# A hybrid attention/SSM layer: up projection of two blocks at a time by one level of Strassen's scheme, down summed in PSUM beside late attention

## The chip, the cores and the metric

The kernel runs on one core of one Trainium2 chip. The metric is the device time of one execution in microseconds. The engines are named as in the profile: PE (TensorE), PEld (its weight loads), DVE (VectorE), ACT (ScalarE), POOL (GpSimd) and SP (SyncE, which issues most DMAs).

## The reference, cut to what matters

One layer on 2048 tokens of 1024 channels, all in float32. Attention has 8 heads of 64, the state space model 32 groups of 16 channels, and the FFN 2816 channels.

```python
h = rmsnorm(x, g_mix) * (1.0 + sc_m) + sh_m
q, k, v, f_logit, u = split(h @ w_in)
attn = rmsnorm(forgetting_attention(q, k, v, log_sigmoid(f_logit + b_fgate)), g_attn_out)
ssm = rmsnorm(s5_ssm(u, ...), g_ssm_out)
x = x + gt_m * (concatenate([attn, ssm]) @ w_out)
h = rmsnorm(x, g_ffn) * (1.0 + sc_f) + sh_f
gate_pre, val = split(h @ w_up)                     # w_up: 1024 x (2 * 2816)
gate_pre = causal_dwconv(gate_pre, conv_w, conv_b)  # width 3, over tokens
x = x + gt_f * ((silu(gate_pre) * val) @ w_down)    # w_down: 2816 x 1024
return rmsnorm(x, g_final)
```

## The kernel before

Channels lie on partitions and tokens along the free axis. The 2048 tokens are four blocks of 512 (TB). A float32 product is made from two float32r parts of each factor: `hi` is a rounded copy (ACT, L65 for weights) and `lo` the rest (DVE subtraction, L66), and three matmuls (hi*hi, hi*lo, lo*hi) stand for one. One unit of work for TensorE is therefore three matmuls of 128 x 128 weights against 512 columns.

The program runs in stages. First come the input projections and the conditioning vector (to about 344 us), then the SSM with attention of block 0 and the late query/key/value projections (to about 657 us). From there on it goes block by block: the mixer's rows and the output projection (`mix_t`, `out_proj`), the norm (`h2_of`), then the FFN. The FFN takes 22 column tiles i in four groups of 6, 6, 5 and 5 (FFG): `up(h2, i)` makes gate and value of tile i with 24 matmuls each (L1154) from 1024-wide weight slots, applies the convolution and silu on DVE and ACT (L1158 to L1168), and splits the result into `act_hi` and `act_lo` (L1170, L1171); after each group `down` multiplies the group's tiles for each of eight output tiles d (L1186 to L1188) and adds them to `yt[d]` in SBUF (L1190). The output projection of block b+1 stands inside the last group of block b. Attention of blocks 1 to 3 runs beside the FFNs: per head, `att_max` finds row maxima (L875, L880), `att_main` makes the scores (L918, L919), the exponentials (L928) with their two parts (`ph` L929, `pl` L930), and the products with the values (L939, L943), and adds up the row sums (`acc`, L938, on POOL and in part on DVE).

The order on each engine is set by a list scheduler when the kernel is built, which follows the program's order and the priorities given in it. Weights come by SP's queue into two raw buffers, and each split has three `w_hi` and three `w_lo` buffers.

## Time and profile before

| what | value |
|---|---|
| time, median of 3 runs | 2708.53 us (2705.61 to 2710.71) |
| span of the profiled execution | 2704.6 us (its own time apart from the span is not listed) |
| granted TensorE clock, mean | 0.983 |
| PE busy | 2614.1 us, 97% |
| DVE busy | 2045.6 us, 76% |
| ACT busy | 1165.7 us, 43% |
| POOL busy | 682.6 us, 25% |
| DMA | 378.99 MB, mean 140 GB/s |

Matmuls overlap in the pipe, so a listed duration of 0.40 us is not what one costs; the distance between two starts is. A group's row gives count, busy time, mean duration in ns, then the idle time of that engine just before the group's instructions and what ended it.

### The profile page before, as it was taken

How to read it: one execution, taken by the hardware profiler on the slowest of the kernel's cores; microseconds unless marked ns; L12 is line 12 of the kernel's file. 1: busy time of each engine (PE TensorE's matmuls, PEld its weight loads, DVE VectorE, ACT ScalarE, POOL GpSimd, SP SyncE). 2: the span in 40 equal slices, each digit the busy share in tenths (PEclk: the TensorE clock that was granted, in tenths of full speed). 3: DMA queues.
4: the chain of work that ended last, by engine and by line, in shares of the span. 5: the costliest groups of instructions: out<-in, count | busy, mean ns of one | idle time of the engine just before them, and what ended most of it. 6: DMA issues, size and time to landing. Idle time of an engine off the chain costs nothing.

```text
span 2704.6 us, 35904 instructions
## 1 busy us (share of the span) xinstructions
PE 2614.1 (97%) x12600; PEld 2121.8 (78%) x12600; DVE 2045.6 (76%) x3366; ACT 1165.7 (43%) x1929; POOL 682.6 (25%) x602
## 2 busy tenths in 40 slices
PE   6889999989999999999999999999999999999998
PEld 3778887868788888888888888787888887888886
DVE  7997789875787877888978688879787655855555
ACT  3322245564454443455545344554454333423223
POOL 3675132130322221234323022343222101100001
PEclk8889999999999999999999999999999999999999
DMA  7367877566344442343443233434433233322222
GB/s 270 118 210 226 290 248 223 172 193 213 94 123 133 129 132 85 126 147 103 145 140 127 100 99 128 137 106 141 134 121 106 83 102 114 134 94 88 98 99 75
DMA packets 217668, 378.99 MB, mean 140 GB/s; under 512 B 22384, under 2 KB 107248, under 8 KB 217488
## 3 DMA queue, kind: packets, MB, share of 16 engines
q1 hardware_dynamic: 216208, 372.50, 42.6%
q0 software_dynamic: 1280, 4.20, 0.4%
q8 instruction: 100, 1.64, 0.2%
q14 instruction: 80, 0.66, 0.1%
HBM read 319.79 MB, written 56.75 MB: 139 GB/s over the span
## 4 chain that ended last, share of the span: by engine, by line
PE 81%; DVE 11%; DMA 4%; issue 2%; SPq 1%; ACT 1%; POOL 0%; POOLq 0%; DVEq 0%; ACTq 0%
PE ff_ps L1154 35%; PE ff_ps L1133 6%; PE ff_ps L1186 6%; PE ff_ps L1187 6%; PE ff_ps L1188 6%; PE sc_ps L919 2%; PE sc_ps L875 2%; PE o_ps L939 2%; PE sc_ps L918 2%; PE o_ps L943 2%; PE vq_ps L399 2%; PE qs_ps L399 2%; PE qs_ps L366 1%; PE vq_ps L366 1%; DVE w_lo L66 1%
## 5 line engine op out<-in xcount | busy, mean ns | idle before, releaser
L65 ACT CAST w_hi<-w_raw 128x1024 fp32r<-128x1024 f32 (+2 forms) x384 | 367.5, 959 | 526.4 <-PE ff_ps L1154 201.8
L66 DVE TENSOR_TENSOR w_lo<-w_raw,w_hi 128x1024 fp32r<-128x1024 f32 (+2 forms) x384 | 443.4, 1156 | 188.7 <-ACT w_hi L65 184.9
L1154 PE MATMUL ff_ps<-h_lo,w_hi 128*128 128x512 f32 x1408 | 558.9, 397 | 0.7 <-DVE h_lo L320 0.7
L1154 PE MATMUL ff_ps<-h_hi,w_lo 128*128 128x512 f32 x1408 | 558.8, 397 | 0.7 <-DVE w_lo L66 0.7
L1154 PE MATMUL ff_ps<-h_hi,w_hi 128*128 128x512 f32 x1408 | 553.2, 395 | 0.0
L938 POOL TENSOR_TENSOR acc<-acc,pf 128x512 f32<-128x512 f32 (+2 forms) x240 | 308.7, 1286 | 565.2 <-ACT pf L928 556.8
L1154 PEld LDWEIGHTS ff_ps<-h_lo,w_hi 128*128 128x128 f32 x1408 | 265.4, 189 | 62.0 <-DVE h_lo L320 1.8
L1154 PEld LDWEIGHTS ff_ps<-h_hi,w_hi 128*128 128x128 f32 x1408 | 265.9, 189 | 59.6 <-issue 0.3
L1154 PEld LDWEIGHTS ff_ps<-h_hi,w_lo 128*128 128x128 f32 x1408 | 265.0, 188 | 59.1 <-DVE w_lo L66 1.2
L930 DVE TENSOR_TENSOR pl<-pf,ph 128x512 fp32r<-128x512 f32 (+1 forms) x320 | 268.5, 848 | 54.2 <-ACT ph L929 53.4
L276 POOL TENSOR_TENSOR sq_acc<-sq_acc,sq 128x512 f32<-128x512 f32 x77 | 124.2, 1614 | 691.1 <-ACT sq L275 688.0
L1187 PE MATMUL ff_ps<-act_lo,w_hi 128*128 128x512 f32 (+1 forms) x719 | 281.2, 391 | 0.0
L1188 PE MATMUL ff_ps<-act_hi,w_lo 128*128 128x512 f32 (+1 forms) x719 | 280.0, 391 | 0.0
L1186 PE MATMUL ff_ps<-act_hi,w_hi 128*128 128x512 f32 (+1 forms) x719 | 280.0, 393 | 0.0
L928 ACT ACTIVATE pf<-sc_ps 128x512 f32<-128x512 f32 (+1 forms) x320 | 170.8, 543 | 229.3 <-PE sc_ps L919 79.7
L880 DVE TENSOR_REDUCE mx<-sc_ps 128x1 f32<-128x512 f32 (+2 forms) x320 | 193.8, 616 | 44.5 <-PE sc_ps L875 27.1
L929 ACT CAST ph<-pf 128x512 fp32r<-128x512 f32 (+1 forms) x320 | 178.1, 567 | 44.5 <-PE o_ps L939 40.3
L1188 PEld LDWEIGHTS ff_ps<-act_hi,w_lo 128*128 128x128 f32 x719 | 135.4, 188 | 29.9 <-issue 0.3
L1187 PEld LDWEIGHTS ff_ps<-act_lo,w_hi 128*128 128x128 f32 x719 | 135.4, 188 | 29.2
L1186 PEld LDWEIGHTS ff_ps<-act_hi,w_hi 128*128 128x128 f32 x719 | 135.1, 188 | 29.4
L1190 DVE SCALAR_TENSOR_TENSOR yt<-ff_ps,mod_tf,yt 128x512 f32<-128x512 f32 (+1 forms) x99 | 71.9, 731 | 93.2 <-PE ff_ps L1188 93.1
L1166 ACT ACTIVATE gs<-cvt 128x512 f32<-128x512 f32 x88 | 55.6, 632 | 186.7 <-DVE cvt L1164 186.4
(455 smaller groups left out, 5032.7 us busy)
## 6 DMA issues: line engine op xcount, KB each, us to landing
w_raw<-in_w_flat SPq DMA_DIRECT2D x258, 512.0 KB
w_raw<-in_w_flat SPq DMA_DIRECT2D x64, 384.0 KB
kb<-kb SPq DMA_DIRECT2D x80, 256.0 KB
vv<-v SPq DMA_DIRECT2D x80, 256.0 KB
w_raw<-in_w_flat SPq DMA_DIRECT2D x64, 320.0 KB
wada<-in_w_ada SPq DMA_DIRECT2D x32, 512.0 KB
ka<-kb SPq DMA_DIRECT2D x80, 128.0 KB
xt<-in_x SPq DMA_DIRECT2D x16, 512.0 KB
```

Source lines behind the costliest of these rows:

```text
L65: nc.scalar.copy(hi[:, :n], raw[:, :n])
L66: nc.vector.tensor_tensor(out=lo[:, :n], in0=raw[:, :n], in1=hi[:, :n].bitcast(F32), op=ALU.subtract)
L880: V.reduce_max(out=mx[:, s, ch : ch + 1], in_=ps[:, 0:n], axis=AX.X)
L928: A.activation(pf[:, cs], ps[:, cs], AF.Exp)
L929: A.copy(ph[:, cs], pf[:, cs])
L930: V.tensor_tensor(out=pl[:, cs], in0=pf[:, cs], in1=ph[:, cs].bitcast(F32), op=ALU.subtract)
L938: eng.tensor_tensor(out=acc[j][:, cs], in0=acc[j][:, cs], in1=pf[:, cs], op=ALU.add)
L1133: T.matmul(ps, lhsT=lt, rhs=rt, start=(i == 0), stop=(i == 23))
L1154: T.matmul(ps, lhsT=lt, rhs=rt, start=(n == 0), stop=(n == 23))
L1186: T.matmul(ps, lhsT=a, rhs=ah[:, ts], start=(c == 0), stop=False)
L1187: T.matmul(ps, lhsT=a, rhs=al[:, ts], start=False, stop=False)
L1188: T.matmul(ps, lhsT=bb, rhs=ah[:, ts], start=False, stop=(c == n - 1))
```

## The change

The FFN is taken for two blocks at a time. For tile i the up weights are a 2 x 2 block matrix (gate or value, first or second half of the 1024 input channels: a11, a12, a21, a22), and the two blocks' activations are the other factor. In place of eight block products, seven are made (`product`, 12 matmuls each, L1365): of a11, a12, s1, s2, s4, s3 and a22 with the operands b11, b21, t1, t2, b22, t3 and t4. The operands are built once per pair of blocks (`up_operands`, on DVE and POOL, split on ACT and DVE); the weight combinations s1 to s4 once per tile (`up_pair`, four additions on POOL, L1347 to L1352). Sums of products are formed partly in PSUM (banks X and Z, L1365 with `first=False`), partly by copies on ACT (L1374, L1379, L1381, L1387) and additions on DVE (L1377, L1383, L1388, L1391). Convolution and silu then work on 1024 tokens at once (L1395 to L1401), the first tap now on ACT, and both parts of the result go to DRAM (L1407).

The program's stages are now: the input stage as before; the SSM with attention of blocks 0 and 1 and the late projections, merged by a written order of TensorE; `up_stage(0)`: `mix_t` and `out_proj` of blocks 0 and 1, the operands, 22 `up_pair`; `down_stage(0)`: down of blocks 0 and 1, each output tile summed over all 22 tiles in one PSUM bank and evicted once (L1416), with the activations reloaded from DRAM, while attention of blocks 2 and 3 stands between its steps in a written order of TensorE; `up_stage(1)`; `down_stage(1)`, down of blocks 2 and 3. In the last group of block 3 four output tiles are cut in token halves, where three were.

DVE, in the FFN, before: one column tile of one block (`cvt` and `gs` are the convolution's tiles, 512 tokens; `rs_v` and `rs_i` belong to a norm).

```order
L66 TENSOR_TENSOR w_lo<-w_raw,w_hi 128x1024
L1160 COPY carry<-gs 128x2
L1162 TENSOR_SCALAR cvt<-gs,cv 128x512
L1163 SCALAR_TENSOR_TENSOR cvt<-gs,cv,cvt 128x512
L1164 SCALAR_TENSOR_TENSOR cvt<-gs,cv,cvt 128x512
L1167 SCALAR_TENSOR_TENSOR cvt<-gs,cvt 128x512
L984 COPY ss_att<-sc_ps 128x4
L1158 COPY gs<-carry 128x2
L122 TENSOR_SCALAR rs_v<-ss_att 128x4
L1168 SCALAR_TENSOR_TENSOR cvt<-cvt,ff_ps 128x512
```

DVE in the changed kernel, a column tile of two blocks in the first up stage (`s_11880` and `s_11881` are the tiles s1|s2 and s4|s3 of the next column tile, `v_raw` its second weight slot, `vz` the value branch).

```order
L73 TENSOR_TENSOR w_lo<-s_11880,w_hi 128x1024
L1396 SCALAR_TENSOR_TENSOR cvt<-gs,cv,cvt 128x1024
L1397 SCALAR_TENSOR_TENSOR cvt<-gs,cv,cvt 128x1024
L73 TENSOR_TENSOR w_lo<-s_11881,w_hi 128x1024
L1388 TENSOR_TENSOR vz<-up_x,vz 128x512
L1391 TENSOR_TENSOR vz<-up_y,vz 128x512
L1400 SCALAR_TENSOR_TENSOR cvt<-gs,cvt 128x1024
L1377 TENSOR_TENSOR gs<-up_y,gs 128x512
L1401 SCALAR_TENSOR_TENSOR vz<-cvt,vz 128x1024
L73 TENSOR_TENSOR w_lo<-v_raw,w_hi 128x512
L1384 COPY gs<-bcol 128x2
L1405 TENSOR_TENSOR al<-vz,ah 128x1024
```

The weight splits of the next tile now stand between the steps of this tile's convolution, and the split of a22 (`v_raw`) stands behind all of them; in the tile before and after it, it stands ahead of L1401.

TensorE in the changed kernel, the seam between two column tiles in the first up stage (`up_x_11344` is bank X of the tile that ends, `up_x_11483` of the next; `w_hi_11334` is a part of s4|s3, `w_hi_11457` of a11|a12).

```order
L1365 MATMUL up_z_11345<-hh_hi_9589,w_lo_11335 128x512
L1365 MATMUL up_x_11483<-hh_hi_9163,w_hi_11457 128x512
L1365 MATMUL up_x_11483<-hh_lo_9164,w_hi_11457 128x512
L1365 MATMUL up_x_11344<-hh_hi_9597,w_hi_11334 128x512
L1365 MATMUL up_x_11344<-hh_lo_9598,w_hi_11334 128x512
L1365 MATMUL up_x_11344<-hh_hi_9597,w_lo_11335 128x512
```

The first two matmuls of the next tile stand ahead of the last product, t3, of this one. Within a tile the products stand as b11, b21, t1, t2, t4, b22, t3.

TensorE in `down_stage(0)` of the changed kernel (L1456 to L1458 are a down step, the other rows attention of block 2 or 3).

```order
L1456 MATMUL acc_ps<-act,w_hi 128x512
L1457 MATMUL acc_ps<-act,w_hi 128x512
L1458 MATMUL acc_ps<-act,w_lo 128x512
L1001 MATMUL sc_ps<-qb,kb 128x512
L1002 MATMUL sc_ps<-qa_12721,ka_12729 128x512
L1027 MATMUL o_ps<-ph,vv 128x512
L1031 MATMUL o_ps<-pl,vv 128x512
L949 MATMUL sc_ps<-ka_12728,qa_12722 128x512
L1456 MATMUL acc_ps<-act,w_hi 128x512
L1457 MATMUL acc_ps<-act,w_hi 128x512
L1458 MATMUL acc_ps<-act,w_lo 128x512
```

Down steps alone fill the places between attention's matmuls, where up, down and out_proj did before.

The diff, cut to its core:

```diff
-    def load(self, off, n, hi, lo):
-        nc = self.nc
-        raw = self.pool.tile([P, WSLOT], F32, name="w_raw", tag="w_raw", bufs=2)
-        src = self.flat[off : off + P * n].rearrange("(p n) -> p n", p=P)
-        nc.sync.dma_start(raw[:, :n], src)
-        nc.scalar.copy(hi[:, :n], raw[:, :n])
-        nc.vector.tensor_tensor(out=lo[:, :n], in0=raw[:, :n], in1=hi[:, :n].bitcast(F32), op=ALU.subtract)
-
-    def get(self, off, n):
-        hi = self.pool.tile([P, WSLOT], F32R, name="w_hi", tag="w_hi", bufs=3)
-        lo = self.pool.tile([P, WSLOT], F32R, name="w_lo", tag="w_lo", bufs=3)
-        self.load(off, n, hi, lo)
-        return hi, lo
+    def raw(self, off, n, raw=None):
+        if raw is None:
+            raw = self.pool.tile([P, WSLOT], F32, name="w_raw", tag="w_raw", bufs=2)
+        src = self.flat[off : off + P * n].rearrange("(p n) -> p n", p=P)
+        self.last = self.nc.sync.dma_start(raw[:, :n], src)
+        return raw
+
+    def split(self, raw, n, hi=None, lo=None):
+        nc = self.nc
+        if hi is None:
+            hi = self.pool.tile([P, WSLOT], F32R, name="w_hi", tag="w_hi", bufs=3)
+            lo = self.pool.tile([P, WSLOT], F32R, name="w_lo", tag="w_lo", bufs=3)
+        nc.scalar.copy(hi[:, :n], raw[:, :n])
+        nc.vector.tensor_tensor(out=lo[:, :n], in0=raw[:, :n], in1=hi[:, :n].bitcast(F32), op=ALU.subtract)
+        return hi, lo
+
+    def split_parts(self, raws):
+
+        hi = self.pool.tile([P, WSLOT], F32R, name="w_hi", tag="w_hi", bufs=3)
+        lo = self.pool.tile([P, WSLOT], F32R, name="w_lo", tag="w_lo", bufs=3)
+        for j, raw in enumerate(raws):
+            self.split(raw, 512, hi[:, j * 512 : (j + 1) * 512], lo[:, j * 512 : (j + 1) * 512])
+        return hi, lo
...
-    def up(h2, i):
-        pss = []
-        for br in range(2):
-            wh, wl = weights.get(*up_slots[2 * i + br])
-...
+        free = 1 if s == 0 else 0
+        mt = mix_t(b0, "row_a", lambda k: hh.get(free))
+        mt1 = mix_t(b1, "row_b", lambda k: hh.get(free) if k < 4 else hh.get(2))
+        xa, acc_a = out_proj(b0, mt, "row_a")
+        one = h_rows(xa, acc_a, mix_ps)
+        f1 = [one(k) for k in range(8)]
+        ops = {"b11": [split_h(f1[k], parts=hh.get(0)) for k in range(4)],
+               "b21": [split_h(f1[k], parts=hh.get(0)) for k in range(4, 8)]}
+        xb, acc_b = out_proj(b1, mt1, "row_b")
+        one = h_rows(xb, acc_b, ff_ps)
+        f2 = {}
+
+        def comb(E, out, a, b):
+            E.tensor_tensor(out=out, in0=a, in1=b, op=ALU.subtract)
+            return out
+
+        t1 = []
+        for k in range(4):
+            f2[k] = one(k)
+            t1.append(comb(V, f1[k], f2[k], f1[k]))
+        ops["t1"] = [split_h(f, parts=hh.get(1)) for f in t1]
+        t2 = []
+        for k in range(4):
+            f2[4 + k] = one(4 + k)
+            t2.append(comb(G, t1[k], f2[4 + k], t1[k]))
+        ops["t2"] = [split_h(f, parts=hh.get(1)) for f in t2]
+        ops["b22"] = [split_h(f2[4 + k], parts=hh.get(0)) for k in range(4)]
+        t3 = [comb(V, f2[k], f2[4 + k], f2[k]) for k in range(4)]
+        ops["t3"] = [split_h(f, parts=hh.get(1)) for f in t3]
+        t4 = [comb(G, f1[4 + k], f1[4 + k], t2[k]) for k in range(4)]
+        ops["t4"] = [split_h(f, parts=hh.get(2)) for f in t4]
+        return ops
...
+    def up_pair(s, i, ops, up, ups, cv):
+
+
+        HW = 512
+        g_raw = weights.raw(*up_slots[2 * i])
+        g_hi, g_lo = weights.split(g_raw, 2 * HW)
+        v_raw = None if i == 0 else up.tile([P, 2 * HW], F32, name="v_raw", tag="v_raw", bufs=2)
+        v_raw = weights.raw(*up_slots[2 * i + 1], v_raw)
+        a11, a12 = g_raw[:, 0:HW], g_raw[:, HW : 2 * HW]
+        a21, a22 = v_raw[:, 0:HW], v_raw[:, HW : 2 * HW]
+        if i == 0:
+            s1, s2 = h_f(), h_f()
+        else:
+            s12, s43 = (up.tile([P, 2 * HW], F32, name=nm, tag="sw", bufs=2) for nm in ("s12", "s43"))
+            s1, s2 = s12[:, 0:HW], s12[:, HW : 2 * HW]
+        G.tensor_tensor(out=s1, in0=a21, in1=a22, op=ALU.add)
+        G.tensor_tensor(out=s2, in0=s1, in1=a11, op=ALU.subtract)
+        s12_hi, s12_lo = weights.split_parts((s1, s2)) if i == 0 else weights.split(s12, 2 * HW)
+        s4, s3 = (h_f(), h_f()) if i == 0 else (s43[:, 0:HW], s43[:, HW : 2 * HW])
+        G.tensor_tensor(out=s4, in0=a12, in1=s2, op=ALU.subtract)
+        G.tensor_tensor(out=s3, in0=a11, in1=a21, op=ALU.subtract)
+        s43_hi, s43_lo = weights.split_parts((s4, s3)) if i == 0 else weights.split(s43, 2 * HW)
+        v_hi, v_lo = weights.split(a22, HW)
...
+        gs = up.tile([P, 2 * TB + 2], F32, name="gs", tag="gs", bufs=2)
+        vz = up.tile([P, 2 * TB], F32, name="vz", tag="vz", bufs=2)
+        ga, gb = gs[:, 2 : TB + 2], gs[:, TB + 2 : 2 * TB + 2]
+        va, vb = vz[:, 0:TB], vz[:, TB : 2 * TB]
+        X, Z = bank("x", 2), bank("z", 1)
+        product(X, (g_hi, g_lo), 0, "b11")
+        A.copy(ga, X)
+        Y = bank("y", 2)
+        product(Y, (g_hi, g_lo), HW, "b21")
+        V.tensor_tensor(out=ga, in0=Y, in1=ga, op=ALU.add)
+        product(Z, (s12_hi, s12_lo), 0, "t1")
+        A.copy(vb, Z)
+        product(X, (s12_hi, s12_lo), HW, "t2", False)
+        A.copy(gb, X)
+        product(Z, (s43_hi, s43_lo), 0, "b22", False)
+        V.tensor_tensor(out=gb, in0=Z, in1=gb, op=ALU.add)
+        V.tensor_copy(gs[:, 0:2], carry[:, i, :])
+        V.tensor_copy(carry[:, i, :], gs[:, 2 * TB : 2 * TB + 2])
+        product(X, (s43_hi, s43_lo), HW, "t3", False)
+        A.copy(va, X)
+        V.tensor_tensor(out=vb, in0=X, in1=vb, op=ALU.add)
+        Y2 = bank("y", 2)
+        product(Y2, (v_hi, v_lo), 0, "t4")
+        V.tensor_tensor(out=va, in0=Y2, in1=va, op=ALU.add)
+
+        n = 2 * TB
+        t = up.tile([P, n], F32, name="cvt", tag="cvt", bufs=1)
+        A.activation(t, gs[:, 0:n], AF.Identity, scale=cv[:, i, 0:1], bias=cv[:, i, 3:4])
+        V.scalar_tensor_tensor(out=t, in0=gs[:, 1 : n + 1], scalar=cv[:, i, 1:2], in1=t, op0=ALU.mult, op1=ALU.add)
+        V.scalar_tensor_tensor(out=t, in0=gs[:, 2 : n + 2], scalar=cv[:, i, 2:3], in1=t, op0=ALU.mult, op1=ALU.add)
+
+        A.activation(gs[:, 0:n], t, AF.Tanh, scale=0.5)
+        V.scalar_tensor_tensor(out=t, in0=gs[:, 0:n], scalar=1.0, in1=t, op0=ALU.add, op1=ALU.mult)
+        V.scalar_tensor_tensor(out=vz, in0=t, scalar=0.5, in1=vz, op0=ALU.mult, op1=ALU.mult)
+        ah = up.tile([P, n], F32R, name="ah", tag="ah", bufs=1)
+        al = up.tile([P, n], F32R, name="al", tag="al", bufs=1)
+        A.copy(ah, vz)
+        V.tensor_tensor(out=al, in0=vz, in1=ah.bitcast(F32), op=ALU.subtract)
+        for j, a in enumerate((ah, al)):
+            Q.dma_start(act_d[s][i][:, :, j, :].rearrange("b p n -> p b n"),
+                        a.rearrange("p (b n) -> p b n", b=2).bitcast(F32))
...
+        for half in range(2):
+            ds = range(4 * half, 4 * half + 4)
+            pss = {d: dps.tile([P, 512], F32, name="acc_ps", tag="acc", bufs=4) for d in ds}
+            c0 = 0
...
+                        for c in range(n):
+                            ah, al = act[c0 + c][:, 0, ts], act[c0 + c][:, 1, ts]
+                            a, bb = wh[:, c * P : (c + 1) * P], wl[:, c * P : (c + 1) * P]
+                            st = g == 0 and c == 0
+                            sp_ = c == n - 1 and (last or tail and half == 1 and g == len(FFG) - 2)
+                            T.matmul(pss[d][:, ts], lhsT=a, rhs=ah, start=st, stop=False, skip_group_check=cut)
+                            T.matmul(pss[d][:, ts], lhsT=a, rhs=al, start=False, stop=False, skip_group_check=cut)
+                            T.matmul(pss[d][:, ts], lhsT=bb, rhs=ah, start=False, stop=sp_, skip_group_check=cut)
+                            yield
+                            step += 1
+                            if step == 6 and norm_late:
+                                norm_late.pop()()
+                        if last:
+                            evict(d, pss[d], ts, V if cut else G)
...
+            downs = itertools.chain(*(down(b, ap, dps, misc, b == NB - 1) for b in (2 * s, 2 * s + 1)))
+            if late:
+                with tc.manual_schedule(engines={mybir.EngineType.PE}):
+                    heads = attention(late, lag=2, lead=4, gap=2)
+                    next(heads)
+                    for _ in range(26):
+                        next(downs)
+                    n = 0.0
+                    for _ in heads:
+                        n += 1.16
+                        while n >= 1:
+                            next(downs, None)
+                            n -= 1
+                    run(downs)
...
-    for b in range(1, NB):
-        attention(b)
-    for b in range(NB):
-        i = 0
-        for g, n in enumerate(FFG):
-            act = [up(h2, i + c) for c in range(n)]
-...
+    up_stage(0, ExitStack(), ExitStack(), mix_ctx.close)
+    down_stage(0, (2, 3))
+    up_stage(1, ExitStack(), ExitStack())
+    down_stage(1)
```

586 lines of the change are left out of this document (354 added, 232 removed).

## The prediction

> **What bounds the kernel now.** I read the page first: the busy line, the slices, the chain.
>
> ```profile
> span 2704.6 us, 35904 instructions
> PE 2614.1 (97%) x12600; PEld 2121.8 (78%) x12600; DVE 2045.6 (76%) x3366; ACT 1165.7 (43%) x1929; POOL 682.6 (25%) x602
> PE   6889999989999999999999999999999999999998
> DVE  7997789875787877888978688879787655855555
> PE 81%; DVE 11%; DMA 4%; issue 2%; SPq 1%; ACT 1%; POOL 0%; POOLq 0%; DVEq 0%; ACTq 0%
> PE ff_ps L1154 35%; PE ff_ps L1133 6%; PE ff_ps L1186 6%; PE ff_ps L1187 6%; PE ff_ps L1188 6%; PE sc_ps L919 2%; PE sc_ps L875 2%; PE o_ps L939 2%; PE sc_ps L918 2%; PE o_ps L943 2%; PE vq_ps L399 2%; PE qs_ps L399 2%; PE qs_ps L366 1%; PE vq_ps L366 1%; DVE w_lo L66 1%
> ```
>
> TensorE holds the end, and the up projection alone (L1154) is 35% of the chain. The view by windows says how evenly; its columns are the window, its length, then busy time of PE, weight loads, DVE, ACT, POOL, the granted clock, the DMA share and GB/s.
>
> ```profile
> 344.00:660.00 316.00, 301.58 (x1798) 249.12 (x1796) 253.66 (x466) 163.26 (x315) 78.13 (x82) 0.98 0.66 208
> 660.00:750.00 90.00, 85.47 (x368) 65.65 (x367) 63.67 (x100) 43.22 (x70) 25.50 (x21) 0.94 0.36 115
> 1200.00:1650.00 450.00, 449.66 (x2045) 362.82 (x2044) 368.11 (x554) 215.90 (x350) 128.23 (x94) 1.00 0.39 125
> 2106.00:2650.00 544.00, 543.73 (x2367) 439.35 (x2367) 314.92 (x481) 182.46 (x247) 25.11 (x17) 1.00 0.30 100
> ```
>
> From 750 to 2650 us TensorE is all but never idle (449.66 of 450 us in the third row). But DVE is at 368 of 450 us where attention runs beside the FFN (82%) and at 315 of 544 (58%) after it: it has some slack, not much. What one matmul costs is its start distance, read from the timeline, not its 0.40 us of listed duration:
>
> ```profile
> 2449.70 0.39 PE L1154 MATMUL ff_ps<-h_hi,w_hi 128*128 128x512 f32 x1
> 2449.93 0.40 PE L1154 MATMUL ff_ps<-h_lo,w_hi 128*128 128x512 f32 x1
> 2450.16 0.40 PE L1154 MATMUL ff_ps<-h_hi,w_lo 128*128 128x512 f32 x1
> 2450.40 0.39 PE L1154 MATMUL ff_ps<-h_hi,w_hi 128*128 128x512 f32 x1
> ```
>
> That is 0.70 us for three, 0.2333 each.
>
> **What goes.** A pair of blocks needs 7 products of 12 matmuls per column tile, 84 in place of 96; over 22 tiles and two pairs that is 528 of 4224 matmuls: 528 x 0.2333 = **-123 us**, if TensorE stays fed. Everything below asks whether it does. Three of four evictions of down (L1190) go too, and the up weights' splits fall from 176 of 1024 to the equal of 154, but on engines that were not the bound.
>
> **The up stage's loop.** One up pair is 84 x 0.2333 = 19.6 us of TensorE. The rows that price its other work (DVE, then ACT, then POOL):
>
> ```profile
> L66 DVE TENSOR_TENSOR w_lo<-w_raw,w_hi 128x1024 fp32r<-128x1024 f32 x256 | 323.9, 1266 | 152.8 <-ACT w_hi L65 149.1 <-PE o_ps L939 0.2
> L253 DVE SCALAR_TENSOR_TENSOR ada_acc<-wada,sil,ada_acc 128x1024 f32<-128x1024 f32 x28 | 38.9, 1390 | 6.3 <-DMA wada<-in_w_ada 6.1
> L317 DVE TENSOR_TENSOR h_lo<-h_f,h_hi 128x512 fp32r<-128x512 f32 x28 | 20.7, 740 | 9.9 <-ACT h_hi L316 9.9
> L958 DVE TENSOR_TENSOR at<-o_ps,at 64x512 f32<-64x512 f32 x32 | 21.9, 685 | 7.9 <-ACT at L957 7.5
> L1160 DVE COPY carry<-gs 128x2 f32<-128x2 f32 x88 | 28.3, 321 | 0.0
> L1158 DVE COPY gs<-carry 128x2 f32<-128x2 f32 x88 | 24.4, 277 | 4.0 <-DMA kb<-qk_lo 1.7 <-DMA kb<-qk_hi 1.5
> L65 ACT CAST w_hi<-w_raw 128x1024 fp32r<-128x1024 f32 x256 | 268.1, 1048 | 336.1 <-PE ff_ps L1154 158.2 <-PE ff_ps L1187 66.4 <-PE ff_ps L1133 42.2
> L938 POOL TENSOR_TENSOR acc<-acc,pf 128x512 f32<-128x512 f32 x144 | 209.4, 1454 | 384.7 <-ACT pf L928 378.6 <-PE vq_ps L1107 4.4
> ```
>
> DVE per pair: four 1024-wide subtractions (three w_lo, one al) at 1.27, one 512 wide at 0.74, four 1024-wide scalar_tensor_tensor with two SBUF inputs at 1.39 (L253 is the only row of that shape), four PSUM additions at 0.69, two copies 0.60: 14.7 us of 19.6, 75%. POOL has four additions at 1.45, 5.8 us. No engine is over 19.6, so by sums nothing is lost. By order something is. The split weights have three buffers (L70, L71, L78, L79 of the changed file), and a pair makes four; so the cast of the next s1|s2 takes the buffer of this pair's s4|s3, which its last product, t3, frees. In the order of the changed file t3 runs after two matmuls of the next pair. From t3's end TensorE has 10 + 12 + 12 + 12 + 1 = 47 matmuls, 11.0 us, to the first one that needs the low part of the next a22 (t4). In that time, in DVE's fixed order: cast 1.05, w_lo of s1|s2 1.27, two convolution steps 2.78, w_lo of s4|s3 1.27, two PSUM additions 1.37, L1400 1.39, the gate addition 0.69, L1401 1.39, w_lo of a22 0.74: 11.95. Every second pair has another order: cast 1.05, w_lo 1.27, addition of gb 0.69, ACT's L1395 1.05, then 2.78, 1.27, 1.37, 1.39, 0.69 and 0.74: 12.3. Four or five hand-overs between engines cost some 0.04 each (ACT's cast at L1170 in the timeline below starts that long after DVE's L1168). So 12.1 and 12.5 stand against 11.0: TensorE waits about 1.35 us per pair. 44 x 1.35 = **+59 us**. Bounds: 0, if the operations are 10% shorter (10.9); 3.3 per pair, +147, if each meets POOL (rival B).
>
> ```profile
> 1361.51 0.67 DVE L1168 SCALAR_TENSOR_TENSOR cvt<-cvt,ff_ps 128x512 f32<-128x512 f32 x1
> 1362.22 0.62 ACT L1170 CAST act_hi<-cvt 128x512 fp32r<-128x512 f32 x1 [0.71 <-DVE cvt L1168]
> 1363.41 1.39 POOL L938 TENSOR_TENSOR acc<-acc,pf 128x512 f32<-128x512 f32 x1 [3.38 <-ACT pf L928]
> 1363.58 1.77 DVE L1171 TENSOR_TENSOR act_lo<-cvt,act_hi 128x512 fp32r<-128x512 f32 x1
> ```
>
> **The operand stages.** Before, out_proj of blocks 1 to 3 lay inside the FFN of the block ahead. Now both out_proj, the norms and 28 operand splits stand alone ahead of each up stage. After the second out_proj's last matmul the way to the operands is: eviction, square, addition and rsqrt, about 6 us; then on DVE eight rows at 0.74 (L331), eight differences at about 0.76, and 20 low parts at 0.74 (L317).
>
> ```profile
> L1136 DVE SCALAR_TENSOR_TENSOR row<-ff_ps,mod_tm,row 128x512 f32<-128x512 f32 x32 | 23.7, 748 | 47.8 <-PE ff_ps L1133 47.8
> L331 DVE SCALAR_TENSOR_TENSOR h_f<-row,mod_gf,vq_ps 128x512 f32<-128x512 f32 x24 | 17.4, 738 | 0.3 <-PE vq_ps L290 0.2
> ```
>
> That is 27 us on DVE, 33 with the front; TensorE has in that time only the first pair's b11 and b21 (5.6 us) and the products as they come (14 us). The unhidden part is between 33 + 2.8 - 19.6 = 16 and all 33; I take 26, nearer the upper end, since both DVE and POOL make the differences. At a stage's start I add 5. The first stage replaces the 4.5 us that TensorE idles in 660 to 750, so **+27**; the second also has the norm of block 1's output on its way (eight rows, 7 us): **+38**. Bounds 10 and 35 each. If the list scheduler had let pair 0 start on more than b11 and b21, this would be less.
>
> **Late attention beside down.** Attention of blocks 2 and 3 stands beside down steps of three matmuls, 1.16 for each attention step. DVE there, from rows of its parts: of 224 pl at 512, 176 belong to blocks 2 and 3 (8 heads x 4 key tiles x (2 + 3) whole ones and 16 diagonal ones).
>
> ```profile
> L930 DVE TENSOR_TENSOR pl<-pf,ph 128x512 fp32r<-128x512 f32 x224 | 208.3, 936 | 40.2 <-ACT ph L929 39.7
> L880 DVE TENSOR_REDUCE mx<-sc_ps 128x1 f32<-128x512 f32 x224 | 151.2, 683 | 32.1 <-PE sc_ps L875 27.1 <-PE sc_ps L879 4.5
> L66 DVE TENSOR_TENSOR w_lo<-w_raw,w_hi 128x768 fp32r<-128x768 f32 x64 | 63.5, 994 | 12.3 <-ACT w_hi L65 12.3
> L66 DVE TENSOR_TENSOR w_lo<-w_raw,w_hi 128x640 fp32r<-128x640 f32 x64 | 56.0, 879 | 23.7 <-ACT w_hi L65 23.5
> ```
>
> pl 165 + 31 for the narrower ones (half of their rows' 61), mx 120 + 22, row sums and head ends about 60, weight splits for some 260 of 352 down steps 44, evictions and the norm 15: about 457 us. TensorE, at start distance, has 182 us of down (780 matmuls) and about 256 of attention in the same stretch, 438. DVE is the longer by about 20, and with 5 for the fill this is **+25**; bounds 0 (pl at 0.68, as it is where POOL is quiet) and +60.
>
> **The rest.** Attention of block 1 joins the SSM stage, DVE 254 + about 110 in some 385 us: near the bound, charged at nothing, since TensorE has the longer sum; +20 if that cover is gone. Activations now go through DRAM; in the first half of down of block 2 or 3 fall 22 x 0.52 = 11.5 MB of them, 5.8 MB of weights (half of 2816 x 1024 x 4 bytes) and 2 MB of residual, in 264 matmuls x 0.2333 = 62 us: about 313 GB/s against the 208 of the SSM row. SP's queue issues the next group's activations behind the second weight of a group. **+6**, between 0 and 15. The end (last token halves) is as before.
>
> **Sum.** -123 + 59 + 27 + 38 + 25 + 6 = +32 on the profiled span of 2704.6: 2736.6. The runs' median is 3.9 above that span; so 2740.
>
> **Rivals.**
>
> A, the saving arrives: the up pairs run at 19.6 us, because the durations I used are means over collided operations (pl has a mean of 0.936, and single ones in the timeline take 0.68). -123 + 0 + 27 + 38 + 25 + 6 = -27; with the operand stages and late attention at half, -72. Time 2636 to 2682, about 2660. For it: TensorE was fed to within 1 us in 450 at 82% DVE. Against: there the weights came in two-product units with no buffer freed as late as t3's.
>
> B, POOL's four additions per pair collide with DVE's chain, which is where the order puts them. In the timeline row above act_lo took 1.77 us in place of its mean of 0.77 while POOL's addition ran, 1.0 more. If two of the four fall into the chain, 44 x 2 x 1.0 = +88: about 2828. For it: they start when the splits just named free their buffers, so beside L1396 to L1400. Against: additions on DVE that read PSUM did not stretch (L1168 at 0.67), and the mean over all pl is only 0.26 above 0.68.
>
> The Trainium skill (SBUF — State Buffer, Terms) says that DVE and GpSimd share a port pair that is locked for a whole instruction, so that the loser fully blocks. The L1171 row agrees: it ends 0.55 us after POOL's addition ended, about the length of one free operation. By that rule the price of B is a whole POOL instruction per collision, 1.45 in place of 1.0, and B would end near 2868; this speaks against putting the combinations of the weights on POOL.
>
> C, the change of order in the two down stages costs more than it hides: DVE in late attention at +60 and the act reload at +15, with no loss in the up loop: -123 + 65 + 75 = +17, 2725.
>
> **Chances.** Forecast (up loop late by 0.7 to 2.4 us a pair, or C): 0.48, its own range 2712 to 2790. A: 0.40. B: 0.12. A measurement here tells about 0.2% from no change, 2703 to 2714. A gives all of faster, 0.40; the seam between A and the forecast gives 0.07; slower 0.53. The range for 8 in 10 is 2640 to 2800: it leaves out the low end of A and most of B.
>
> **What would show it.** Start distances of t1 to t4 in the up stage: gaps of 1 to 2 us ahead of the matmul that takes w_lo of a22 (L1365, released by DVE's L73) prove the loop; 19.6 us per pair proves A. L1396, L1397 and L1400 far above 1.39 us beside POOL's L1347 to L1352 prove B. TensorE's idle after each second out_proj shows the operand term; DVE over 95% in late attention shows that one. The forecast falls if the up stages take 431 us each.

## The result: 4.7% slower

The changed kernel takes 2837.39 us (median of 4 runs, 2834.53 to 2839.07) against 2707.8 us before (2705.61 to 2710.71): a ratio of 1.047, 95% interval 1.0454 to 1.0487. The forecast had the sign, but 2740 us and an upper bound of 2800 were too low. The page of the changed kernel:

```profile
span 2837.4 us, 35672 instructions
PE 2573.9 (91%) x12087; PEld 2057.7 (73%) x12087; DVE 2043.3 (72%) x3097; ACT 1281.8 (45%) x2034; POOL 1008.5 (36%) x803
PE   6888989988997999999798988899888999999997
DVE  7988699876757777777487887795678777773233
PEclk8889999998998999999898999999888999999999
PE 63%; DVE 15%; DMA 8%; issue 8%; ACT 2%; POOL 2%; SPq 1%; ACTq 0%; POOLq 0%; DVEq 0%
```

TensorE has 513 matmuls fewer in the trace and is busy for only 40 us less; its share of the chain falls from 81% to 63%, and no engine has taken its place: DVE's busy time is the same as before. The view by windows shows the stages (busy time of PE, weight loads, DVE, ACT, POOL, then the granted clock, DMA share and GB/s):

```profile
344.00:793.00 449.00, 400.44 (x2236) 318.22 (x2234) 358.36 (x666) 249.68 (x476) 158.01 (x148) 0.95 0.59 180
793.00:889.00 96.00, 94.98 (x428) 76.79 (x429) 61.55 (x84) 47.57 (x71) 25.25 (x16) 1.00 0.48 169
889.00:1353.00 464.00, 438.45 (x1861) 352.23 (x1860) 349.80 (x379) 213.59 (x272) 168.00 (x99) 0.96 0.29 101
1353.00:1950.00 597.00, 524.68 (x2274) 401.88 (x2275) 459.87 (x655) 325.94 (x561) 272.87 (x217) 0.93 0.50 159
1950.00:2104.00 154.00, 139.23 (x621) 111.80 (x620) 91.50 (x180) 67.78 (x109) 32.92 (x21) 0.94 0.49 170
2104.00:2567.00 463.00, 437.84 (x1861) 351.92 (x1859) 349.04 (x378) 213.28 (x272) 163.02 (x93) 0.97 0.29 101
2567.00:2837.40 270.40, 251.66 (x1140) 205.72 (x1140) 88.77 (x148) 64.65 (x93) 17.75 (x17) 0.97 0.57 199
```

In order: the SSM with attention of blocks 0 and 1; both output projections; up pairs; down of blocks 0 and 1 beside late attention; the second pair of output projections; up pairs; down of blocks 2 and 3. A "loss" below is the sum over a stretch of the distance from each matmul's start to the next one's, less what that matmul takes at full rate (0.233 us for 512 columns and in proportion; worked out from the starts in both traces).

| stretch | loss before, us | loss after, us | difference |
|---|---|---|---|
| input stage (to 344) | 93 | 95 | +2 |
| SSM stage (344 to 660; 344 to 793) | 69 | 132 | +63 |
| operands of the first pair (660 to 750; 793 to 955) | 14 | 34 | +20 |
| FFN with attention (750 to 2650) | 31 | none of this kind | -31 |
| up pairs, both stages | | 4 | +4 |
| late attention beside down (1353 to 1950) | | 134 | +134 |
| operands of the second pair (1950 to 2150) | | 55 | +55 |
| the rest (2650 to the end; 2567 to the end) | 7 | 14 | +7 |

Together +254; with the 123 us of matmuls that went, +131, where the spans differ by 2837.4 - 2704.6 = 132.8. So the matmuls were saved in full, and twice as much was lost elsewhere.

**The up pairs run at full rate.** Three pieces of the chain, each the start of 24 matmuls on bank X, at a distance of two column tiles:

```profile
1112.63 5.58 PE up_x L1365 x24
1151.65 5.58 PE up_x L1365 x24
1190.66 5.58 PE up_x L1365 x24
```

39.0 us for two tiles is 19.5 a tile, where 84 x 0.2333 is 19.6. The loop that I counted at 1.35 us a tile isn't there. The timeline beside the second piece (ACT, DVE and POOL) shows why:

```profile
1151.52 1.05 ACT L72 CAST w_hi<-s 128x1024 fp32r<-128x1024 f32 x1 [4.09 <-PE up_y L1365]
1153.96 2.23 POOL L1347 TENSOR_TENSOR s<-v_raw 128x512 f32<-128x512 f32 x1 [12.35 <-DVE w_lo L73]
1154.76 1.05 ACT L72 CAST w_hi<-s 128x1024 fp32r<-128x1024 f32 x1 [1.05 <-PE up_x L1365]
1155.07 2.21 DVE L1397 SCALAR_TENSOR_TENSOR cvt<-gs,cv,cvt 128x1024 f32<-128x1024 f32 x1
1157.20 2.32 DVE L73 TENSOR_TENSOR w_lo<-s,w_hi 128x1024 fp32r<-128x1024 f32 x1
```

The cast of the next s1|s2 (the first row) is released by bank Y, that is by product t4, before t3 begins; t3 frees the buffer of s4|s3, 3.2 us later, and that is needed last. So the buffers go round in another way than I had it. The collisions of rival B are real: POOL's addition takes 2.2 us and the DVE operations beside it 2.2 and 2.3. The groups say the same for the whole run: L1397 and the low part of the combinations meet POOL's additions in a part of the tiles and are drawn out, L1396, which mostly starts just ahead of one, is not:

```profile
L73 DVE TENSOR_TENSOR w_lo<-s,w_hi 128x1024 fp32r<-128x1024 f32 x84 | 125.4, 1493 | 36.4 <-ACT w_hi L72 36.0 <-PE up_x L1365 0.4
L1397 DVE SCALAR_TENSOR_TENSOR cvt<-gs,cv,cvt 128x1024 f32<-128x1024 f32 x44 | 75.9, 1725 | 1.6
L1396 DVE SCALAR_TENSOR_TENSOR cvt<-gs,cv,cvt 128x1024 f32<-128x1024 f32 x44 | 57.4, 1305 | 22.9 <-ACT cvt L1395 22.9
```

A mean hides that two cases are mixed in it: 21 of the 44 L1397 run beside an addition of POOL's and take 2.21 us each, the other 23 take 1.29. But DVE is busy for 350 of 464 us there, and behind the operands TensorE waits for none of it (2 us of loss from 955 to 1353).

**Late attention is where the time went.** The view of waits, TensorE, 1400 to 1950 us (total, times, longest):

```profile
PE o_ps L1027 <- DVE at L1051: 16.6, 13, 2.2
PE sc_ps L962 <- DVE mneg L958: 12.9, 12, 3.1
PE o_ps L1031 <- DVE pl L1013: 6.9, 7, 4.2
PE sc_ps L949 <- DMA ka<-cum: 6.3, 3, 4.1
PE sc_ps L1002 <- DMA qa<-rrow: 5.4, 2, 4.3
```

L1051 empties a head's one output bank when the head ends, `mneg` is the negated maximum of a head's rows, pl the low part of the exponentials; ka and qa are a head's operands, which come by DMA. They are many causes and none is large. DVE's 460 us in this stage are what the forecast counted (457); it is busy for 77% of the stage, TensorE for 88%. And a wait costs more than its length. The timeline of TensorE after the longest wait for pl:

```profile
1715.47 0.40 PE L1027 MATMUL o_ps<-ph,vv 128*128 128x512 f32 x1
1720.08 0.80 PE L1031 MATMUL o_ps<-pl,vv 128*128 128x512 f32 x1 [4.21 <-DVE pl L1013]
1720.67 0.63 PE L1456 MATMUL acc_ps<-act,w_hi 128*128 128x512 f32 x1
1721.10 0.63 PE L1457 MATMUL acc_ps<-act,w_hi 128*128 128x512 f32 x1
1721.53 0.63 PE L1458 MATMUL acc_ps<-act,w_lo 128*128 128x512 f32 x1
```

After it the starts are 0.43 us apart in place of 0.23. Of the 134 us lost in this stage some 95 are gaps over 0.2 us, and some 40 are matmuls that started 0.06 to 0.2 us late, about half of that (20 us) while the granted clock was at 0.50, as it was behind the longest of the gaps; the mean granted clock of the window is 0.93.

### The profile page after: what moved, and what is told of

Its sections match the earlier page's. It is cut to its first block, busy times and chain, and to the rows that moved or that the text cites. A ratio compares the mean times of both kernels' runs of the same rounds, so it can differ in the third digit from the quotient of the medians.

```text
span 2837.4 us, 35672 instructions
## 1 busy us (share of the span) xinstructions
PE 2573.9 (91%) x12087; PEld 2057.7 (73%) x12087; DVE 2043.3 (72%) x3097; ACT 1281.8 (45%) x2034; POOL 1008.5 (36%) x803
## 4 chain that ended last, share of the span: by engine, by line
PE 63%; DVE 15%; DMA 8%; issue 8%; ACT 2%; POOL 2%; SPq 1%; ACTq 0%; POOLq 0%; DVEq 0%
PE up_x L1365 13%; PE up_z L1365 8%; PE up_y L1365 8%; PE ff_ps L1275 6%; PE acc_ps L1456 4%; PE acc_ps L1458 4%; PE acc_ps L1457 4%; PE sc_ps L949 2%; PE o_ps L1027 2%; DMA w_raw<-in_w_flat 2%; DVE pl L1013 2%; DVE mx L954 2%; PE sc_ps L1002 1%; PE sc_ps L1001 1%; DVE w_lo L73 1%
## 5 line engine op out<-in xcount | busy, mean ns | idle before, releaser
L73 DVE TENSOR_TENSOR w_lo<-w_raw,w_hi 128x1024 fp32r<-128x1024 f32 (+3 forms) x254 | 283.8, 1119 | 233.9 <-ACT w_hi L72 213.9
L72 ACT CAST w_hi<-w_raw 128x1024 fp32r<-128x1024 f32 (+3 forms) x254 | 230.9, 910 | 368.5 <-DMA w_raw<-in_w_flat 126.7
L1456 PE MATMUL acc_ps<-act,w_hi 128*128 128x512 f32 (+1 forms) x724 | 292.9, 405 | 10.9 <-DMA act<-act 5.1
L1458 PE MATMUL acc_ps<-act,w_lo 128*128 128x512 f32 (+1 forms) x724 | 288.2, 399 | 0.4 <-DVE w_lo L73 0.3
L1457 PE MATMUL acc_ps<-act,w_hi 128*128 128x512 f32 (+1 forms) x724 | 288.1, 398 | 0.0
L315 POOL TENSOR_TENSOR sq_acc<-sq_acc,sq 128x512 f32<-128x512 f32 x76 | 122.7, 1615 | 455.4 <-ACT sq L314 454.3
L1347 POOL TENSOR_TENSOR s<-v_raw 128x512 f32<-128x512 f32 x42 | 74.8, 1780 | 388.1 <-DVE w_lo L73 370.0
L1365 PE MATMUL up_x<-hh_lo,w_hi 128*128 128x512 f32 x528 | 208.5, 395 | 0.0
L1365 PE MATMUL up_x<-hh_hi,w_hi 128*128 128x512 f32 x528 | 206.9, 392 | 0.0
L1365 PE MATMUL up_x<-hh_hi,w_lo 128*128 128x512 f32 x528 | 202.8, 397 | 0.0
L1012 ACT CAST ph<-pf 128x512 fp32r<-128x512 f32 (+1 forms) x320 | 181.2, 566 | 19.6 <-PE o_ps L1027 9.3
L1456 PEld LDWEIGHTS acc_ps<-act,w_hi 128*128 128x128 f32 x724 | 142.5, 197 | 41.5 <-DVE vz L1391 4.3
L1458 PEld LDWEIGHTS acc_ps<-act,w_lo 128*128 128x128 f32 x724 | 140.0, 194 | 31.6 <-DVE w_lo L73 1.3
L1457 PEld LDWEIGHTS acc_ps<-act,w_hi 128*128 128x128 f32 x724 | 141.0, 195 | 28.4
L1365 PE MATMUL up_z<-hh_hi,w_hi 128*128 128x512 f32 x352 | 139.5, 396 | 15.3 <-ACT hh_hi L355 15.3
L1027 PE MATMUL o_ps<-ph,vv 128*128 128x512 f32 (+1 forms) x320 | 133.8, 418 | 19.7 <-DVE at L1051 19.3
```

The costliest lines, as they stand in the source:

```text
L72: nc.scalar.copy(hi[:, :n], raw[:, :n])
L73: nc.vector.tensor_tensor(out=lo[:, :n], in0=raw[:, :n], in1=hi[:, :n].bitcast(F32), op=ALU.subtract)
L1012: A.copy(ph[:, cs], pf[:, cs])
L1027: T.matmul(o_ps[0][:, cs], lhsT=vt[:, i, :], rhs=ph[:, cs], start=first, stop=False)
L1365: T.matmul(ps, lhsT=lt, rhs=rt, start=(first and n == 0), stop=(n == 11), skip_group_check=not first)
L1456: T.matmul(pss[d][:, ts], lhsT=a, rhs=ah, start=st, stop=False, skip_group_check=cut)
```

## The experiments

Each time is a single measurement. The kernel before took 2710 to 2717 us beside them, so differences under some 8 us are not read as anything. Times are set against the 2837 us of the changed kernel.

**TensorE's order set by the scheduler in the late stage.**

```diff
-                with tc.manual_schedule(engines={mybir.EngineType.PE}):
+                if True:
                     heads = attention(late, lag=2, lead=4, gap=2)
```

> The changed kernel, with TensorE's written order taken away in the stage of down(0,1) beside attention of blocks 2 and 3: the list scheduler sets it there. In the changed kernel this stage takes about 612 us (1353 to 1965), 136 us more than its matmuls at their start distance. Theory 1 (the written order makes TensorE wait in line: for mneg, for the head's end at L1051, for pl): the stage loses at least 60 us less, 2837 falls to 2780 or below. Theory 2 (DVE is too slow there, drawn out by POOL): no order helps, within 15 us of 2837. Theory 3 (the scheduler knows less than the written order): slower, by up to 40.

Measured: 2895.5, 58 us slower. The written order is not the cause; it is better than what the scheduler finds. The trace also shows where attention loses: the scheduler set most down steps first. From 1357 to 1615 us, with 792 down matmuls and 319 of attention, the loss is 15 us; in the 185 us behind that, with 509 matmuls of attention and 18 of down, it is 90.

**POOL's row sum additions left out for earlier blocks' keys.**

```diff
-            else:
+            elif j or b < 2 or ch == b:
                 eng.tensor_tensor(out=acc[j][:, cs], in0=acc[j][:, cs], in1=pf[:, cs], op=ALU.add)
```

> The changed kernel without POOL's row sum additions (L1021) for the keys of earlier blocks in attention of blocks 2 and 3, so the row sums of these blocks are not the reference's; every other instruction stays. POOL's 164 or so additions leave the late stage. Theory 2 (POOL collides with DVE's pl and draws it out to 1.02 us): pl falls to about 0.70, the late stage loses 50 us less or more, 2787 or below. Theory 1 (written order): pl is shorter too, but the waits at the heads' ends stay: 2810 to 2837.

Measured: 2812.2, 25 us less. In the late stage (1353 to 1950 us) the 512-wide pl was, in the changed kernel and then in this one:

```profile
L1013 DVE TENSOR_TENSOR pl<-pf,ph 128x512 fp32r<-128x512 f32 x176 | 180.2, 1026 | 38.2 <-ACT ph L1012 37.6
```

```profile
L1013 DVE TENSOR_TENSOR pl<-pf,ph 128x512 fp32r<-128x512 f32 x176 | 126.4, 720 | 59.9 <-ACT ph L1012 59.8
```

POOL's collisions draw pl out by 0.3 us, 54 us of DVE in all, but only 25 reach the end. The Trainium skill (SBUF — State Buffer, the section on SBUF's two separate sides) says that a DVE operation with two SBUF inputs and a GpSimd one that reads SBUF lock each other out; these rows agree in that pl is shorter with fewer additions on POOL.

**No low part of the exponentials in late attention.**

```diff
-            V.tensor_tensor(out=pl[:, cs], in0=pf[:, cs], in1=ph[:, cs].bitcast(F32), op=ALU.subtract)
+            if b < 2:
+                V.tensor_tensor(out=pl[:, cs], in0=pf[:, cs], in1=ph[:, cs].bitcast(F32), op=ALU.subtract)
+            else:
+                pl = ph
```

> The changed kernel without the low part of the exponentials in attention of blocks 2 and 3: DVE makes no pl there, and TensorE multiplies ph in its place, as often as before. So these two blocks' attention is less precise, and DVE has 224 subtractions (some 200 us) less in the late stage. Theory 2 (DVE's rate sets the stage): the stage comes near its matmuls' start distance, 2837 - 100 = 2737 or below. Theory 1 (order, head ends, DMA of the heads): at most 40 us go, 2797 or above.

Measured: 2805.5, 32 us less. From the windows view of this kernel, the late stage:

```profile
1353.00:1930.00 577.00, 522.67 (x2348) 408.70 (x2347) 273.15 (x443) 333.60 (x576) 253.82 (x220) 0.95 0.54 172
```

DVE is down to 273 of 577 us. The last product of attention starts at 1913 us in place of 1950, and up to there the stage still loses some 94 us in place of 134. So DVE's rate carries a part of the loss, but it alone does not bound the stage.

**The Strassen products undone, the rest kept.**

```diff
         product(X, (g_hi, g_lo), 0, "b11")
+        product(X, (g_hi, g_lo), HW, "b21", False)
         A.copy(ga, X)
         Y = bank("y", 2)
-        product(Y, (g_hi, g_lo), HW, "b21")
-        V.tensor_tensor(out=ga, in0=Y, in1=ga, op=ALU.add)
...
```

> The changed kernel with the Strassen products undone and all else kept (stages, pairs of blocks, DRAM for the activations, late attention beside down): eight products of 12 matmuls per column tile, each result summed in one PSUM bank, no combinations of weights or operands, two weight splits per tile. If the up stages of the changed kernel are set by TensorE alone, this adds 528 x 0.2333 = 123 us and takes back what the simpler operands save, 10 to 40: 2837 + 83 to 113 = 2920 to 2950. If DVE's chain set them (my forecast's loop), the difference is under 60: below 2897.

Measured: 2924.1, 87 us more. So the scheme by itself, with its combinations and longer operand stages, gains 87 us; what cost time is the grouping of the stages that it was put into.

**Attention of block 1 left out.**

```diff
-            merge((attention((0, 1), lag=2, lead=0, gap=1, ahead=2), 104, 0.0, 0.9), (late, 2 * 96, 0.05, 1.0))
+            merge((attention((0,), lag=2, lead=0, gap=1, ahead=2), 40, 0.0, 0.9), (late, 2 * 96, 0.05, 1.0))
...
```

> The changed kernel without attention of block 1 (its mixer rows are taken from block 0's, so block 1's and the later results are not the reference's): the SSM stage keeps attention of block 0 and the late projections, as it was before the change. The stage took 449 us, 132 of them beyond its matmuls' start distance; the same work before the change lost 69, without attention of block 1, whose matmuls are some 70 us. Theory A (block 1's attention has too little other TensorE work beside it): the stage gives back 70 and another 50 or more, 2837 falls to 2717 or below. Theory B (the merged written order itself, or the late projections in it, is what costs): only the 70, 2760 to 2770.

Measured: 2736.4, 101 us less: 70 for the matmuls and some 31 of loss, between the two theories of the expectation. The SSM stage then loses 99 us, where before the change it lost 69 with the same work. TensorE's longest wait in it is for the late projections' operands, not for attention:

```profile
PE qs_ps L443 <- ACT h_hi L355: 10.7, 4, 6.7
```

So half of the 63 us there is block 1's attention, and half comes with the merged late projections or their order, which these runs do not separate.

**The scheduler's order in the SSM stage.**

```diff
-        with tc.manual_schedule(engines={mybir.EngineType.PE}):
+        if True:
             late = itertools.chain(qkv_late(2, qs_ps), qkv_late(3, qs_ps))
```

> The changed kernel with TensorE's written order taken away in the SSM stage alone (attention of blocks 0 and 1 with the late projections); the list scheduler sets it there. Theory B (the written order costs the 63 us that the stage lost beyond before): 30 or more are given back, 2807 or below. Theory A (too little cover for block 1's attention): no gain, 2830 to 2890, as in the late stage, where the scheduler's order was 58 us slower.

Measured: 2849.3, 12 us more. The scheduler does no better here either.

**High priority for the ends of heads.**

```diff
+            with tc.high_priority():
                 A.copy(at[mine], o_ps[0][other])
                 V.tensor_tensor(out=at[mine], in0=o_ps[0][mine], in1=at[mine], op=ALU.add)
```

and the same around mneg and rrow.

> The changed kernel with the few DVE and ACT operations at a head's end (o_ps to at, L1050 and L1051; mneg L958; rrow L964) given high priority with the list scheduler, so that they stand earlier in DVE's queue. In the late stage TensorE waited 16.6 us for L1051 and 12.9 us for mneg. If these waits are queueing on DVE: 20 to 45 us less with the slow matmuls behind each wait, 2792 to 2817. If DVE's rate is the limit, the wait moves to pl: within 12 of 2837.

Measured: 2840.0, no difference. But the priority moved nothing: by their names and shapes, the instructions of DVE and ACT stand in the same order as without it in the whole late stage. So the run does not tell whether a head's end waits in DVE's queue. The waits are as they were; in this kernel's view of waits (its L1054 is L1051 of the changed kernel, L1029 is L1027):

```profile
PE o_ps L1029 <- DVE at L1054: 15.6, 13, 2.2
```

**One step less between scores and values.**

```diff
-                    heads = attention(late, lag=2, lead=4, gap=2)
+                    heads = attention(late, lag=1, lead=4, gap=2)
```

> The changed kernel with one step in place of two between a key tile's scores and its product with the values in the written order of the late stage (lag 1): half the cover for exp, its two parts and their queues. If cover is what the late stage lacks: at least 40 us slower, 2877 or above. If the stage is set by DVE's rate or by transfers: within 15 of 2837.

Measured: 2937.7, 100 us more. TensorE now waits 98 times for pl in the late stage:

```profile
PE o_ps L1031 <- DVE pl L1013: 68.9, 98, 6.0
```

So the TensorE work that stands between a score and its use, its cover, matters a great deal.

**One step more.**

```diff
-                    heads = attention(late, lag=2, lead=4, gap=2)
+                    heads = attention(late, lag=3, lead=4, gap=2)
```

> The changed kernel with three steps in place of two between scores and values in the late stage's written order (lag 3), the buffers as they are. Lag 1 cost 100 us. If cover is still short at lag 2: the waits for pl (L1031, 10.7 us) and part of the slow matmuls behind them go, and DVE's queue is less in TensorE's way: 15 to 50 us less, 2787 to 2822. If lag 2 is enough and the head ends and transfers are what is left: within 10 of 2837.

Measured: 2827.5, 10 us less, at the edge of what one run tells. TensorE's wait for L1051 fell from 16.6 to 4.6 us, and that for pl is no longer among the largest, yet little of it reached the end. So with two steps the way from scores to values seems nearly covered, and more delay alone doesn't replace work.

**Two banks for a head's output, two for scores.**

```diff
-                    o_ps.append(att_ps[-1].tile([P, 512], F32, name="o_ps", tag="o", bufs=1))
+                    o_ps.append(att_ps[-1].tile([P, 512], F32, name="o_ps", tag="o", bufs=2 if b > 1 else 1))
...
-                sc_extra.append(opened(st, "sc_ps", bufs=1, space=PSUM))
```

> The changed kernel with two PSUM banks for the output of a head in the late stage in place of one, and two in place of three for scores. TensorE waits 16.6 us there for DVE to empty the one bank (L1051). If the single bank is the cause: these waits go with the slow matmuls behind them, 15 to 30 us less, 2807 to 2822. If DVE is simply behind at a head's end, the wait moves to scores (L949, L1001) and mneg: 2827 or above, and more than 2847 if the third bank for scores was needed.

Measured: 2852.4, 15 us more. The wait for L1051 went, and others came in its place in the late stage:

```profile
PE sc_ps L1001 <- DVE mx L954: 8.5, 13, 1.7
PE sc_ps L949 <- DVE mx L954: 8.2, 7, 2.4
PE sc_ps L949 <- ACT pf L1011: 8.0, 20, 1.5
```

**More work for DVE in the up pairs.**

```diff
         s43_hi, s43_lo = weights.split_parts((s4, s3)) if i == 0 else weights.split(s43, 2 * HW)
+        if i:
+            V.tensor_tensor(out=s43_lo[:, 0 : 2 * HW], in0=s43, in1=s43_hi[:, 0 : 2 * HW].bitcast(F32), op=ALU.subtract)
```

> The changed kernel with the 1024-wide low part of s4|s3 made twice by DVE in every column tile but the first of a stage (42 extra subtractions of 1.2 to 2.3 us, right in the chain that my forecast took for the limit). By the forecast's loop, with no slack, each counts in full: 42 x 1.3 = 55 us or more, 2892 or above. By the trace of the changed kernel, where the up stages run at their matmuls' start distance and DVE is idle for some 5 us per tile: under 10 us, 2847 or below.

Measured: 2837.8, no difference. In the first up stage DVE went from 350 us to this, for nothing:

```profile
889.00:1353.00 464.00, 441.97 (x1875) 354.81 (x1874) 393.88 (x398) 212.43 (x271) 187.96 (x99) 0.96 0.29 99
```

44 us more on DVE, at the place that my loop took for the limit, are covered. The loop has a slack of at least 2 us a tile.

**Late attention left out, in both kernels.** In the changed kernel:

```diff
-                    heads = attention(late, lag=2, lead=4, gap=2)
-                    next(heads)
+                    heads = ()
...
```

> The changed kernel with attention of blocks 2 and 3 left out (their mixer rows are taken from blocks 0 and 1, so these blocks' results are not the reference's): down of blocks 0 and 1 stands alone in the late stage, with the same loads at its start. Attention's matmuls there are about 256 us at their start distance. Theory A (attention without enough other matmuls loses time): 256 and another 90 or more go, 2491 or below. Theory D (the stage's losses are down's own, the activations' loads at its start above all): 256 and at most 40 go, 2541 or above.

In the kernel before:

```diff
-    for b in range(1, NB):
-        attention(b)
+    attention(1)
...
```

> The kernel before with the same attention of blocks 2 and 3 left out in the same way (results not the reference's). Where attention lies beside up, down and the output projection it should cost its matmuls alone by theory A: 256 us and 0 to 25 more, 2427 to 2452. If it lost as much there, 340 or more go.

Measured: spans of 2475.8 in place of 2837.4, and of 2432.4 in place of 2704.6. The same attention costs 362 us in the changed kernel and 272 before, where its matmuls are some 256. Down alone, with the same loads at its start, loses only 23 us (1353 to 1590). So it is attention beside down that loses: 90 us more than beside the whole FFN.

**60 down steps ahead of attention, with lag 3.**

```diff
-                    for _ in range(26):
+                    for _ in range(60):
```

> The changed kernel with lag 3 and 60 down steps in place of 26 ahead of attention's first scores in the late stage, so that the heads' loads come when the first group's activations are in. Lag 3 alone gave 2827.5. Theory D: the waits of some 16 us for ka, qa and mneg at 1376 to 1406 and the slow matmuls behind them go, 2800 to 2815. Theory A: the cover that is used up at the start is missing at the end, within 8 of 2827.

Measured: 2821.4, 6 us less than with lag 3 alone, which is not read as anything: the loads at the start are no large part.

**Each down step of blocks 0 and 1 of six matmuls in place of three.**

```diff
                             T.matmul(pss[d][:, ts], lhsT=a, rhs=ah, start=st, stop=False, skip_group_check=cut)
+                            if b < 2:
+                                T.matmul(pss[d][:, ts], lhsT=a, rhs=al, start=False, stop=False, skip_group_check=cut)
+                                T.matmul(pss[d][:, ts], lhsT=bb, rhs=ah, start=False, stop=False, skip_group_check=cut)
+                                T.matmul(pss[d][:, ts], lhsT=a, rhs=al, start=False, stop=False, skip_group_check=cut)
```

> The changed kernel with each down step of blocks 0 and 1 made of six matmuls in place of three (the first products counted twice, so the results are not the reference's): twice as much TensorE work between attention's steps, nothing more on DVE, ACT, POOL or DMA. At their start distance these 1056 matmuls are 246 us. Theory A: the losses of the late stage fall from 136 by 60 to 110, so only 136 to 186 us come on top, 2973 to 3023. Theory D, or DVE's rate in its own right: the losses stay, 3070 to 3090.

Measured: a span of 2990.5, 153 us more for 246 us of added matmuls. The late stage (1353 to 2090 here) loses 42 us in place of 134, and the largest waits of the changed kernel are nearly gone:

```profile
PE o_ps L1031 <- DVE pl L1013: 1.8, 1, 1.8
PE o_ps L1027 <- DVE at L1051: 1.6, 3, 0.9
```

With the work of attention on DVE, ACT, POOL and DMA unchanged, more TensorE work beside it removes 92 us of loss. That is the cause: each attention step has 1.16 down steps beside it, 0.8 us of matmuls, and that is too little cover for what attention does on the other engines. Which of its ways lacks the most is not shown. A third step between scores and values gained 10 us; leaving out POOL's additions gained 25 and pl 32; the heads' ends, maxima and loads each show waits of 5 to 17 us, and the two runs that changed how long TensorE waits for L1051, lag 3 and the second output bank, gained 10 us and lost 15.

## Why the prediction was right and wrong

**What goes**: right. 528 matmuls at their start distance were saved, and undoing the products alone costs 87 us, the 123 less the longer operand stages and the rest.

**The up stage's loop** (+59): wrong, it is 0, as rival A had it, with the 19.6 us per pair that were to show it (19.5). The step that failed is "so the cast of the next s1|s2 takes the buffer of this pair's s4|s3, which its last product, t3, frees". The trace shows it released by t4, some 3 us ahead of t3's end; and 44 us of added DVE work in that chain of the first up stage changed nothing. Rival A's reason was another, operations shorter than I had them, and that is not so: the low part of the combinations took 1.49 us on average and L1397 1.73, against 1.27 and 1.39. I had deduced which of three buffers is reused from the order of the requests in the code.

**Rival B**: its mechanism is there (L1397 at 2.21 beside POOL against 1.29 without), its price is nought, since the chain that it lengthens has slack. The row given against it, L1168 at 1361.51, was no test: it ended 1.2 us before POOL's addition began. What it was to show holds in the changed kernel, though: L1388, which reads PSUM, took 0.68 us in the 40 cases beside an addition of POOL's and in the other four.

**The operand stages** (+27 and +38): about right. They lose 20 and 55 us more; the sum, 75, is 10 over the 65 of the forecast. TensorE waits there as foreseen for the operands' parts on ACT and DVE. Two rows of its waits in the second such stage:

```profile
PE up_z L1365 <- ACT hh_hi L355: 7.7, 1, 7.7
PE mx_ps L1249 <- DVE row L1245: 5.9, 2, 5.2
```

The second row is `mix_t`, whose rows are now loaded only behind the end of late attention (the last head's result is stored at 1956.2 us, the first row's load is issued at 1956.6); the forecast had not named it.

**Late attention beside down** (+25): the mechanism was wrong and the term five times too small, 134. DVE's sum was right (460 against 457 forecast). TensorE's came to 463 (597 less the loss) against 438, since 302 down steps lay in the stage and not 260. The step that failed is the one from the sums to the time: "DVE is the longer by about 20" took the longer of two sums for the time. And it is not that the sums were nearly equal: with pl taken off DVE, 187 us less there, the gain was 32 us only, and some 94 us were still lost beside a DVE that was less than half busy. In place of the longer sum the runs show too little cover: engines that hand work to each other at every step wait for each other in turn when TensorE has too little other work beside it. One step less between scores and values cost 100 us, twice the down matmuls took 92 us off the loss, and the same attention costs 362 us beside down alone against 272 beside the whole FFN. Which hand-over lacks cover the most stays open.

**The rest**: attention of block 1 "charged at nothing, since TensorE has the longer sum" is the same error, +63, over the +20 that I had set as its bound; half of it is block 1's attention, for the other half only the merged projections' operands are seen waiting, and the cause stays open. The 31 us that the FFN itself lost before were not in the sum; they went. Loads in the last stage and the end: +6 forecast, +7.

In sum the forecast erred by -59 on a loss that isn't there, +109 on late attention, +63 on the SSM stage, +10 on the operands and -31 on what the FFN had lost: +92 of the 101 by which the spans differ from 2736.6. The sign came out right by luck, since the errors on attention were the larger: without the loop, the same sum would have said 27 us faster. Rival C named the place, at +60 in place of 134.

## What to carry to other kernels

Work that is saved on the engine that bounds a kernel may also have been the cover for something else: before a stage's matmuls are cut or regrouped, ask which latency chain ran beside them, and how much matmul time per step of that chain is left. Where engines hand work to each other at every step, the longer of their sums is a lower bound and not the time, even when the other sum is far shorter; a run with the cover doubled tells at once whether it is that. And which buffer of a rotating pool a tile gets should be read from what releases it in a trace, not from the order of requests.

## What the runs showed of the hardware

A wait of TensorE can be paid twice. After the 4.2 us wait at 1715 us the matmuls started 0.43 us apart for about 5 us; and a shorter one does it too (TensorE's timeline; the starts behind the wait are 0.59 and 0.43 us apart):

```profile
1519.66 0.23 PE L1007 MATMUL sc_ps<-mask_t,identb 128*128 128x128 bf16 x1
1521.70 0.79 PE L1027 MATMUL o_ps<-ph,vv 128*128 128x512 f32 x1 [1.81 <-DVE at L1051]
1522.29 0.63 PE L1031 MATMUL o_ps<-pl,vv 128*128 128x512 f32 x1
1522.72 0.52 PE L949 MATMUL sc_ps<-ka,qa 66*128 66x384 f32 x1
```

The mean granted clock fell from 0.983 to 0.950. The Trainium skill (TensorE: Matmul & The Clock Gate, the part on the HAM clock gate) puts the fall to half clock behind an idle window of about 3.4 us, and 426.7 ns for a cold 512-column matmul; the 0.43 us agree, but here a single wait of 1.8 us was enough. TensorE had run at its full rate for some 10 us before it, with a granted clock of 1.00 (1510 to 1520 us), and the clock was 0.50 from 1522 to 1525 us; two waits of 1.2 and 1.0 us, at 1505.6 and 1508.1 us, had left it at 1.00.
